# Group B's gates with features on partitions, applied behind the transposes; local and context scores of 256 keys in one product

## The chip, the cores and the metric

The kernel runs on one core of a Trainium2 chip. The metric is the device time of one execution in microseconds. A core has a matrix engine (TensorE, "PE" in the profile, with its weight loads as "PEld"), a vector engine (VectorE, "DVE"), an activation engine (ScalarE, "ACT"), a general engine (GpSimd, "POOL") and a queue for transfers (SyncE, "SP"). Matrix products are written to PSUM, which has eight banks of 128 x 512 float32; everything else lives in SBUF.

## The reference

Two layers of a transformer with three groups of attention heads side by side, over 512 latent tokens (a grid of 8 rows by 64 columns) and 256 context tokens, width 1024, head size 64, float32. Cut to what matters:

```python
px = split_cols(hx @ w_in)      # latent; hx is the normalised, modulated input
pc = split_cols(hc @ w_in)      # context, through the same weights
ya, yca = global_gqa(...)          # A: 8 heads, all latent keys and all context keys
yb, ycb = neighbourhood_attn(...)  # B: 8 heads, a clamped 8 x 16 window, a bias, and all context keys
yc_, ycc = window_gqa(...)         # C: 8 heads, keys within 128 tokens, a sink logit, all context keys
ux = jnp.concatenate([ya, yb, yc_], axis=-1) * jax.nn.silu(px[9])
x = x + gate[:, None, :] * (ux @ w_out)
if need_ctx:                       # first layer only
    uc = jnp.concatenate([yca, ycb, ycc], axis=-1) * jax.nn.silu(pc[9])
    cx = cx + gate_c * (uc @ w_out)
```

`px[9]` and `pc[9]` are 1536 columns of gates, 512 for each group. The second layer makes nothing for the context beyond its keys and values.

## The kernel before, in words

Products are made of two rounded halves of every operand, high and low, three products for each (high with high, high with low, low with high), so that float32 accuracy remains. The weights come in pieces of 256 KB on SP's queue; ACT rounds the high half (`split`, L242), DVE or POOL subtracts for the low one (L245).

There are two forms of projection. `proj_t` puts 128 tokens on the partitions of the result: the stationary operand is a tile of 128 tokens, the moving one a weight block of 256 columns, 24 products of 256 columns for a tile, two tiles in a bank (L336). `proj_f` puts 128 features on the partitions: the weights are stationary, the tokens move, 24 products of 512 columns for the latent part and 24 of 256 for the context (L313). Weight blocks are numbered in two tables, `wt` and `wf` (`col_index`).

Heads are worked in pairs (12 pairs, four in each group). `PLAN` lists stages: in each, the attention of one pair is woven on TensorE with the projections that later pairs need (`weave`, with a rough cost for each kind in `time`). Stage `("B", 3)`, for instance, runs attention of B's last pair beside the projections `akv` and `a` 0, and stage `("A", 0)` runs A's first pair beside `ckv` and `c` 0. The instructions so written get a priority by their order, and a planner, with its own estimate of times, fixes the order on every engine and gives each tile a buffer when its first writer is placed; a tile waits until the former holder of its buffer is done. On the chip every engine then follows that order. Projections use two PSUM banks, `pj`, one after the other.

Attention of a pair is made of units, one head each (`NearUnit` in B, `BandUnit` in C, `GlobalUnit` in A, `CtxUnit` for context queries). For a tile of 128 queries a unit makes two products with the context keys and two with the local keys (the high and low half of the keys), into one region of `Sbig`; then DVE adds the bias and finds the maximum, ACT takes the exponential, TensorE transposes the probabilities into `T`, ACT and DVE split them (L793, L1039), and TensorE multiplies them with the values into `Obig`. In `NearUnit` query tiles 1 and 2 have 256 local keys, tiles 0 and 3 have 192. In `BandUnit` tiles 0 and 3 have 256, tiles 1 and 2 have 384.

`finish(c)` ends a pair, in the next stage, behind the last unit's values. It needs the gates (the factor 0.5 of the tanh form is applied there):

- groups A and B: the gates G have tokens on partitions. POOL multiplies G in place with the reciprocal of the softmax sums (L1315, one instruction for each tile of 128 tokens), TensorE transposes, and DVE multiplies the transposed product with the attention output OT into u (L1332).
- group C: the gates (`c_g`) have features on partitions. POOL multiplies a constant of ones with the reciprocals into a tile R in the slot `tR` (L1315), TensorE transposes, DVE multiplies OT with it in place (L1326), and POOL multiplies with G into u (L1328, L1330).

u is then stored by a transfer from ACT's queue (L1340), except for the last three. Slot `tR` has one buffer. It also holds the rotated K and Q of group C (`rope_c`: L966, L974, L976) and group C's V before its transposes (L1001, L1003).

B's gates before: `b_g(m)` makes the gates of two pairs at once by `proj_t`, with a tanh on ACT and a product on DVE for each half bank (`g_silu`, L874, L875).

Of the kernel before, what the change touches and what calls it, by code (L numbers as in the profile page):

```python
# [21 lines left out]
NT = 512  # L22
NCX = 256
NA = NT + NCX
# [5 lines left out]
RPAD = 32  # L30
FT_ORDER = (4, 5, 6, 7, 0, 8, 1, 9, 2, 10, 3, 11)

PLAN = [(None, [("g", 0), ("b", 0), ("v", 0)], (0, 18)),
# [15 lines left out]

CFG = dict(lead=6.0, hp=600, hpf=600, pj=2, T=2, O=1, P=5, qt=5, kt=4, vt=4, gt=3, wh=5, ws=3, pt=3, bm=2, tA=1, OT=1, u=1, tl=1, ab="pj", tR=1, map={}, ada=2, h0=300, h1=1000, a0=9, H=2, hr=0, cp="A", cv="A", w0="D", w1="D", w2=(("D", "D"), ("D", "D")), hb="D", ws_="P")  # L50

WT_A_KV, WT_A, WT_BV, WT_BG = 0, 1, 5, 7
WF_BQ, WF_BK, WF_CQ, WF_CK, WF_CV, WF_CG = 0, 4, 8, 12, 13, 14

SM_C, SM_NW, SM_AB, SM_FW = 0, 16, 32, 80
SM_N = 88
# [710 lines left out]
def mixers(tc, nc, l, last, p1, ps, const, env):  # L767
# [6 lines left out]
    nq = 4 if last else 6  # L774
    ncol = nq * 128
    need_cq = not last
# [7 lines left out]
    def newG():  # L784
        return slot("gt")
# [149 lines left out]
        yield from proj_t(l, WT_BV + m, 6, bank, done, g_["off_tile"])  # L935
        return V

    def b_g(m, bank):
        G = [newG() for _ in range(2)]

        def done(p, t2):
            for x in range(2):
                g_silu(G[x], p, t2, x * 128)

        yield from proj_t(l, WT_BG + m, nq, bank, done)
        return G

    def tables_c():
        for c in range(2):
# [63 lines left out]

    def c_g(i, bank):

        G = p1.tile([128, NA], F32, name="gc", tag="bm", bufs=CFG["bm"])

        def done(p, c0, n):
            th = p1.tile([128, NT], F32, name="th", bufs=1)
            nc.scalar.activation(th[:, 0:n], p, AF.Tanh, scale=0.5)  # L1020
            nc.vector.scalar_tensor_tensor(G[:, c0:c0 + n], th[:, 0:n], 1.0, p, op0=OP.add, op1=OP.mult)

        yield from proj_f(l, WF_CG + i, need_cq, bank, done)
        return G

    def c_pair(i, bank):
        Q = yield from c_q(i, bank)
# [15 lines left out]
    def mul(*args, **kw):  # L1043
        m = nc.tensor.matmul(*args, **kw)  # L1044
        pace["pe"] = m.ins.name
        return m
# [24 lines left out]
    def sbank():  # L1071

        k = third["n"] = (third["n"] + 1) % 3
        return Sbig[:, k * 512:(k + 1) * 512]

    class Unit:

# [86 lines left out]
    class BandUnit(Unit):  # L1164
        def scores(self):
            self.P, self.pos = {}, {}

            place = {1: (128, 128, 512), 2: (768, 1024, 768), 0: (0, 0, 256), 3: (1024, 1280, 1024)}
            for pair in ((1, 2), (0, 3)):
                for i in pair:  # L1170
                    ks = KS[i]
                    nl = 128 * len(ks)
                    s0, loc, cx = place[i]
                    q = self.Q[:, i * 128:(i + 1) * 128]
                    for x in range(2):
                        mul(Sbig[:, cx:cx + 256], q, self.K[:, x, NT:NA],
                                         start=(x == 0), stop=(x == 1), skip_group_check=True)
                        mul(Sbig[:, loc:loc + nl], q, self.K[:, x, ks[0] * 128:ks[0] * 128 + nl],
                                         start=(x == 0 and nl > 256), stop=(x == 1), skip_group_check=True)
                    yield (nl + 256) * 2 / 2400  # L1180
                for i in pair:
                    ks = KS[i]
                    s0, loc, cx = place[i]
                    n = 128 * len(ks) + 256
                    nm = self.stat("negm", i)
                    P = newP()
                    nc.vector.tensor_tensor_reduce(out=P[:, 0:n], in0=Sbig[:, s0:s0 + n], in1=self.bm()(i),  # L1187
                                                   op0=OP.add, op1=OP.min, scale=-1.0,
                                                   scalar=self.sink if self.sink is not None else 3.0e38, accum_out=nm)
# [23 lines left out]
    class NearUnit(Unit):  # L1213
# [9 lines left out]
        def scores(self):  # L1223
            self.P = {}
            for i in (1, 2, 0, 3):
                k0, p0, loc, cx, _ = self.PLAN[i]
                nl = min(256, NT - k0, 128 * i + 192)
                S = sbank()
                q = self.Q[:, i * 128:(i + 1) * 128]
                for x in range(2):  # L1230
                    a = mul(S[:, cx:cx + 256], q, self.K[:, x, NT:NA], start=(x == 0), stop=(x == 1),
                                         skip_group_check=True)
                    b = mul(S[:, loc:loc + nl], q, self.K[:, x, k0:k0 + nl], start=False,
                                         stop=(x == 1), skip_group_check=True)
                    if x == 0:
                        after(b, a.ins.name)
                yield (nl + 256) * 2 / 2400
                n = nl + 256
                nm = self.stat("negm", i)
                P = newP()  # L1240
                if n < 512:
                    z = 0 if p0 else n
                    nc.gpsimd.memset(P[:, z:z + 64], 0.0)
# [50 lines left out]
    def finish(c):  # L1294
# [8 lines left out]
                nc.vector.tensor_add(sums[:, h * 6:h * 6 + nq], sums[:, h * 6:h * 6 + nq], ex[:, h * 6:h * 6 + nq])  # L1303
        rec = p1.tile([128, 2, 6], F32, name="rec", bufs=2)
        nc.vector.reciprocal(rec[:, :, 0:nq], sums.rearrange("p (h t) -> p h t", h=2)[:, :, 0:nq])
        if kind == "C":
            R = slot("tR")
        else:
            R = G
# [1 line left out]
        u = slot("u")  # L1311
        ft = {"A": 0, "B": 4, "C": 8}[kind] + i
        for t in range(nq):
            src = onesw[:, None, :].to_broadcast([128, 2, 64]) if kind == "C" else R[:, t]
            en("fin").tensor_mul(R[:, t], src, rec[:, :, t:t + 1].to_broadcast([128, 2, 64]))  # L1315
        yield 0
        for c0, n in ((0, 4), (4, nq - 4)):
            if not n:
                continue
            T = psT()  # L1320
            for t in range(n):
                turn(T[:, t * 128:(t + 1) * 128],
                                    R[:, c0 + t].rearrange("p h f -> p (h f)"), ident)
            a, b = c0 * 128, (c0 + n) * 128
            if kind == "C":
                nc.vector.scalar_tensor_tensor(OT[:, a:b], OT[:, a:b], 0.5, T[:, 0:b - a], op0=OP.mult, op1=OP.mult)  # L1326
                if c0 == 0:
                    nc.gpsimd.tensor_mul(colmajor(u[:, 0:NT]), rowmajor(OT[:, 0:NT]), colmajor(G[:, 0:NT]))  # L1328
                else:
                    nc.gpsimd.tensor_mul(u[:, a:b], OT[:, a:b], G[:, a:b])  # L1330
# [160 lines left out]

    first = any_bank
    made = {}
    time = dict(akv=15.7, a=15.7 * nq / 6, ckv=15.7, c=2 * tq, b=7.8 + tq, v=15.7, g=15.7 * nq / 6)
    make = dict(akv=lambda i, bank: a_kv(bank), a=a_pair, ckv=lambda i, bank: c_kv(bank), c=c_pair, b=b_qk, v=b_v,
                g=b_g)

# [7 lines left out]
    for pair, items, n_ada in PLAN:  # L1505
        if pair is None and not last:

            items = items[1:] + items[:1]
        if pair is not None:
            kind, i = pair  # L1510
            if kind == "B":
                Q, K = made["b", i]
                prev = units("B", i, Q, K, made["v", i // 2][i % 2], lambda i=i: made["g", i // 2][i % 2], bmb)
# [33 lines left out]
def col_index():  # L1547
# [6 lines left out]
    wt += [3072 + 512 + i * 256 + r(256) for i in range(2)]  # L1554
# [4 lines left out]
    wf += [3072 + 1024 + i * 128 + r(128) for i in range(4)]  # L1559
    return wt, wf  # L1560


# [80 lines left out]
```

## Time and profile before

| | |
|---|---|
| median of 3 runs | 1206.64 us (1205.81 to 1206.85) |
| profiled execution | 1206.79 us |
| its span, first to last instruction | 1204.9 us |
| TensorE busy | 1159.1 us, 96%, 8016 products |
| DVE busy | 766.0 us, 64% |
| ACT busy | 697.7 us, 58% |
| POOL busy | 418.3 us, 35% |
| mean granted TensorE clock | 0.995 |

The busy time of an engine is the time in which at least one of its instructions runs. Products overlap, so the mean duration of one says less than the distance between starts in a run without interruption. "Idle before" tells what ended an empty stretch. A line such as `Sbig<-kt,qt` names the tile written and the tiles read.

### The profile page before, as it was taken

How to read it: one execution, taken by the hardware profiler on the slowest of the kernel's cores; microseconds unless marked ns; L12 is line 12 of the kernel's file. 1: busy time of each engine (PE TensorE's matmuls, PEld its weight loads, DVE VectorE, ACT ScalarE, POOL GpSimd, SP SyncE). 2: the span in 40 equal slices, each digit the busy share in tenths (PEclk: the TensorE clock that was granted, in tenths of full speed). 3: DMA queues.
4: the chain of work that ended last, by engine and by line, in shares of the span. 5: the costliest groups of instructions: out<-in, count | busy, mean ns of one | idle time of the engine just before them, and what ended most of it. 6: DMA issues, size and time to landing. Idle time of an engine off the chain costs nothing.

```text
span 1204.9 us, 21753 instructions
## 1 busy us (share of the span) xinstructions
PE 1159.1 (96%) x8016; PEld 1037.9 (86%) x8016; DVE 766.0 (64%) x1541; ACT 697.7 (58%) x1581; POOL 418.3 (35%) x511
## 2 busy tenths in 40 slices
PE   5999999999999999999999999999999999989997
PEld 3898999998888989988878999989989888878876
DVE  5767566764556656568577895576755655557553
ACT  5446555655656576588423543554666766667552
POOL 1441110234447354376110030212365554546001
PEclk9999999999999999999999999999999999999998
DMA  8552222312223112124086662332321202132152
GB/s 328 203 141 89 78 77 75 121 64 95 80 94 100 54 56 78 49 62 119 27 305 205 196 199 75 94 105 83 106 67 57 68 30 71 36 88 80 35 158 79
DMA packets 60826, 124.22 MB, mean 103 GB/s; under 512 B 7216, under 2 KB 13488, under 8 KB 60720
## 3 DMA queue, kind: packets, MB, share of 16 engines
q1 hardware_dynamic: 54768, 111.96, 29.2%
q10 hardware_dynamic: 5952, 10.88, 2.7%
q8 instruction: 63, 1.03, 0.3%
q14 instruction: 43, 0.35, 0.1%
HBM read 109.05 MB, written 11.14 MB: 100 GB/s over the span
## 4 chain that ended last, share of the span: by engine, by line
PE 83%; DVE 6%; ACT 4%; DMA 3%; issue 3%; POOL 0%; ACTq 0%; SPq 0%; DVEq 0%; POOLq 0%
PE pj L313 19%; PE pj L336 17%; PE Sbig L1044 10%; PE Obig L1044 9%; PE T L1049 9%; PE pj L514 4%; PE T L514 3%; PE Sbig L514 3%; PE T L336 2%; PE Sbig L425 1%; DVE ptl L1039 1%; ACT pth L793 1%; PE pj L425 1%; PE Sbig L336 1%; PE pj L209 1%
## 5 line engine op out<-in xcount | busy, mean ns | idle before, releaser
L1039 DVE TENSOR_TENSOR ptl<-T,pth 128x512 fp32r<-128x512 f32 (+2 forms) x312 | 181.3, 591 | 126.8 <-ACT pth L793 124.9
L793 ACT ACTIVATE pth<-T 128x512 fp32r<-128x512 f32 (+2 forms) x312 | 158.8, 519 | 136.4 <-PE T L1049 123.4
L336 PE MATMUL pj<-wh,hL 128*128 128x256 f32 x896 | 180.0, 287 | 0.1
L313 PE MATMUL pj<-hL,wh 128*128 128x512 f32 x544 | 176.3, 402 | 1.0 <-ACT wh L242 0.6
L1049 PE MATMUL T<-ident,P 128*128 128x128 f32 x1024 | 165.8, 274 | 5.9 <-DVE ptl L1039 3.7
L242 ACT ACTIVATE wh<-ws 128x512 fp32r<-128x512 f32 x192 | 119.6, 629 | 80.9 <-PE pj L313 13.9
L1044 PE MATMUL Sbig<-kt,qt 128*128 128x256 f32 (+1 forms) x864 | 157.0, 309 | 0.9 <-DVE negm L1187 0.7
L245 POOL TENSOR_TENSOR wl<-ws,wh 128x512 fp32r<-128x512 f32 x76 | 98.4, 1300 | 154.3 <-ACT wh L242 141.2
L336 PEld LDWEIGHTS pj<-wh,hL 128*128 128x128 f32 x896 | 144.2, 191 | 2.5 <-issue 0.6
L1049 PEld LDWEIGHTS T<-ident,P 128*128 128x128 f32 x1024 | 123.0, 140 | 19.9 <-DVE ptl L1039 3.9
L1044 PE MATMUL Obig<-pth,vt 128*128 128x256 f32 (+2 forms) x432 | 133.2, 319 | 6.0 <-ACT pth L793 5.2
L1044 PE MATMUL Obig<-ptl,vt 128*128 128x256 f32 (+2 forms) x432 | 132.1, 320 | 3.6 <-DVE ptl L1039 3.1
L1044 PEld LDWEIGHTS Sbig<-kt,qt 128*128 128x128 f32 x864 | 123.7, 190 | 10.2 <-DVE negm L1187 2.2
L336 PE MATMUL pj<-wl,hL 128*128 128x256 f32 x448 | 128.5, 287 | 0.0
L245 DVE TENSOR_TENSOR wl<-ws,wh 128x512 fp32r<-128x512 f32 x116 | 85.2, 741 | 43.3 <-ACT wh L242 39.4
L313 PEld LDWEIGHTS pj<-hL,wh 128*128 128x128 f32 x544 | 96.6, 190 | 17.1 <-ACT wh L242 1.0
L313 PE MATMUL pj<-hL,wl 128*128 128x512 f32 x272 | 107.4, 395 | 0.6 <-DVE wl L245 0.6
L1044 PEld LDWEIGHTS Obig<-pth,vt 128*128 128x128 f32 x432 | 81.9, 190 | 16.6 <-ACT pth L793 9.6
L1044 PEld LDWEIGHTS Obig<-ptl,vt 128*128 128x128 f32 x432 | 81.8, 189 | 14.7 <-DVE ptl L1039 9.6
L1419 POOL TENSOR_TENSOR bm<-wr,bm 128x192 f32<-128x192 f32 (+1 forms) x48 | 40.8, 881 | 142.2 <-DMA bm<-mskB_dram 134.8
L336 PEld LDWEIGHTS pj<-wl,hL 128*128 128x128 f32 x448 | 85.4, 191 | 0.4
L1139 DVE TENSOR_REDUCE negm<-Sbig 128x1 f32<-128x768 f32 x64 | 61.1, 955 | 33.3 <-ACT P L1141 18.2
(334 smaller groups left out, 2510.5 us busy)
## 6 DMA issues: line engine op xcount, KB each, us to landing
ws<-wf_dram SPq DMA_DIRECT2D x72, 256.0 KB, 2.9
ws<-wt_dram SPq DMA_DIRECT2D x72, 256.0 KB, 2.9
ada<-adaw_dram SPq DMA_DIRECT2D x32, 512.0 KB, 5.1
ws<-wo_dram SPq DMA_DIRECT2D x57, 256.0 KB, 2.8
bm<-mskB_dram SPq DMA_DIRECT2D x16, 576.0 KB, 3.9
dw<-adat_dram SPq DMA_DIRECT2D x8, 512.0 KB, 7.3
dots<-adat_dram SPq DMA_DIRECT2D x16, 256.0 KB, 4.1
u<-u ACTq DMA_DIRECT2D x9, 384.0 KB, 3.1
```

Source lines behind the costliest of these rows:

```text
L242: nc.scalar.activation(hi, src, AF.Copy)
L245: eng.tensor_sub(lo, src, hi.bitcast(F32))
L313: paced(nc.tensor.matmul(p[:, 0:n], a[:, r, :], cols(b[kt], c0, n), start=(i == 0), stop=(i == 23)), i)
L336: paced(nc.tensor.matmul(p[:, t * 256:(t + 1) * 256], tok(a[kt], t2 + t), b[:, r, :], start=(i == 0), stop=(i == 23)), i)
L425: mm = nc.tensor.matmul(out, a, b, start=begin, stop=(kt == KT - 1 and i == 2), skip_group_check=True)
L514: mm = nc.tensor.matmul(p[:, 0:n], a[:, r, :], ucols(ua[b][ft], c0, n), start=(ft == FT_ORDER[0] and i == 0), stop=(ft == FT_ORDER[-1] and ...
L793: nc.scalar.activation(out, src, AF.Copy)
L1039: i = nc.vector.tensor_sub(lo[:, 0:n], T[:, 0:n], hi[:, 0:n].bitcast(F32))
L1044: m = nc.tensor.matmul(*args, **kw)
L1049: m = nc.tensor.transpose(*args, **kw)
L1139: nc.vector.tensor_reduce(nm, S, axis=AX.X, op=OP.max, negate=True)
L1419: nc.gpsimd.tensor_add(b, src, b)
```

## The change: what it does

1. `b_g(i)` makes the gates of one pair by `proj_f`, as group C does, from four new weight blocks of 128 features (`WF_BG`) in place of two blocks of 256. ACT's tanh and DVE's product are now one each for 512 latent columns and one each for the 256 context columns. `PLAN` names `g` 0 and 1 in the first stage and 2 and 3 in stage `("B", 2)`.
2. `finish` treats B as it does C: ones times reciprocals into R in the slot `tR`, transposes, OT times R in place on DVE, then u = OT times G on POOL, with plain column order.
3. Where a query tile has 256 local keys, the local and the context keys are read by one product of 512 columns, through an access pattern of two runs of 256 (`beside`). This concerns tiles 1 and 2 of `NearUnit` and tiles 0 and 3 of `BandUnit`; in tile 3 of the latter the second run lies before the first.

```diff
-PLAN = [(None, [("g", 0), ("b", 0), ("v", 0)], (0, 18)),
+PLAN = [(None, [("g", 0), ("g", 1), ("b", 0), ("v", 0)], (0, 18)),
...
-        (("B", 2), [("b", 3), ("g", 1)], (0, 0)),
+        (("B", 2), [("b", 3), ("g", 2), ("g", 3)], (0, 0)),
...
-    def b_g(m, bank):
-        G = [newG() for _ in range(2)]
-
-        def done(p, t2):
-            for x in range(2):
-                g_silu(G[x], p, t2, x * 128)
-
-        yield from proj_t(l, WT_BG + m, nq, bank, done)
+    def gate_f(G, s, bank):
+        def done(p, c0, n):
+            th = p1.tile([128, NT], F32, name="th", bufs=1)
+            nc.scalar.activation(th[:, 0:n], p, AF.Tanh, scale=0.5)
+            nc.vector.scalar_tensor_tensor(G[:, c0:c0 + n], th[:, 0:n], 1.0, p, op0=OP.add, op1=OP.mult)
+
+        yield from proj_f(l, s, need_cq, bank, done)
         return G
+
+    def b_g(i, bank):
+        return (yield from gate_f(newG(), WF_BG + i, bank))
...
+    def beside(k, k0, k1):
+        return bass.AP(tensor=k.tensor, offset=k.offset + k0, ap=[k.ap[0], [k1 - k0, 2], [1, 256]])
...  # BandUnit.scores
+                        if nl == 256:
+                            k0 = ks[0] * 128
+                            mul(Sbig[:, s0:s0 + 512].rearrange("p (a b) -> p a b", a=2), q,
+                                beside(self.K[:, x], *((k0, NT) if loc < cx else (NT, k0))),
+                                start=(x == 0), stop=(x == 1), skip_group_check=True)
+                            continue
...  # NearUnit.scores
+                    if nl == 256:
+                        mul(S[:, 0:512].rearrange("p (a b) -> p a b", a=2), q, beside(self.K[:, x], k0, NT),
+                            start=(x == 0), stop=(x == 1), skip_group_check=True)
+                        continue
...  # finish
-        if kind == "C":
+        if kind in "BC":
             R = slot("tR")
...
-            src = onesw[:, None, :].to_broadcast([128, 2, 64]) if kind == "C" else R[:, t]
+            src = onesw[:, None, :].to_broadcast([128, 2, 64]) if kind in "BC" else R[:, t]
...
-            if kind == "C":
+            if kind in "BC":
                 nc.vector.scalar_tensor_tensor(OT[:, a:b], OT[:, a:b], 0.5, T[:, 0:b - a], op0=OP.mult, op1=OP.mult)
-                if c0 == 0:
+                if c0 == 0 and kind == "C":
                     nc.gpsimd.tensor_mul(colmajor(u[:, 0:NT]), rowmajor(OT[:, 0:NT]), colmajor(G[:, 0:NT]))
...
-    time = dict(akv=15.7, a=15.7 * nq / 6, ckv=15.7, c=2 * tq, b=7.8 + tq, v=15.7, g=15.7 * nq / 6)
+    time = dict(akv=15.7, a=15.7 * nq / 6, ckv=15.7, c=2 * tq, b=7.8 + tq, v=15.7, g=tq)
...
-            items = items[1:] + items[:1]
+            items = items[2:] + items[:2]
```

`c_g` calls `gate_f` too, with nothing else changed; `col_index` and the shapes of `wt` and `wf` follow (7 and 22 blocks in each layer, 9 and 18 before).

More of the change, by code (lines that the diff above doesn't have):

```diff
@@ L50 @@
 CFG = dict(lead=6.0, hp=600, hpf=600, pj=2, T=2, O=1, P=5, qt=5, kt=4, vt=4, gt=3, wh=5, ws=3, pt=3, bm=2, tA=1, OT=1, u=1, tl=1, ab="pj", tR=1, map={}, ada=2, h0=300, h1=1000, a0=9, H=2, hr=0, cp="A", cv="A", w0="D", w1="D", w2=(("D", "D"), ("D", "D")), hb="D", ws_="P")
-WT_A_KV, WT_A, WT_BV, WT_BG = 0, 1, 5, 7
-WF_BQ, WF_BK, WF_CQ, WF_CK, WF_CV, WF_CG = 0, 4, 8, 12, 13, 14
+WT_A_KV, WT_A, WT_BV = 0, 1, 5
+WF_BQ, WF_BK, WF_CQ, WF_CK, WF_CV, WF_CG, WF_BG = 0, 4, 8, 12, 13, 14, 18
 SM_C, SM_NW, SM_AB, SM_FW = 0, 16, 32, 80
@@ L1014, in c_g @@
     def c_g(i, bank):
[L1016 to L1024, printed above, removed]
+        return (yield from gate_f(p1.tile([128, NA], F32, name="gc", tag="bm", bufs=CFG["bm"]), WF_CG + i, bank))
     def c_pair(i, bank):
@@ L1512, in mixers @@
                 Q, K = made["b", i]
-                prev = units("B", i, Q, K, made["v", i // 2][i % 2], lambda i=i: made["g", i // 2][i % 2], bmb)
+                prev = units("B", i, Q, K, made["v", i // 2][i % 2], lambda i=i: made["g", i], bmb)
             else:
@@ L1553, in col_index @@
     wt += [1792 + i * 256 + r(256) for i in range(2)]
-    wt += [3072 + 512 + i * 256 + r(256) for i in range(2)]
     wf = [768 + i * 128 + r(128) for i in range(4)]
@@ L1559, in col_index @@
     wf += [3072 + 1024 + i * 128 + r(128) for i in range(4)]
+    wf += [3072 + 512 + i * 128 + r(128) for i in range(4)]
     return wt, wf
@@ L1616 @@
     w4 = w_in.reshape(2, 8, 128, 4608).transpose(0, 2, 1, 3)
-    wt = np.ascontiguousarray(np.stack([w4[..., i] for i in it], 1).reshape(2, 9, 128, 2, 4, 256)
-                              .transpose(0, 1, 3, 2, 4, 5)).reshape(2, 9, 2, 128, 1024)
-    wf = np.ascontiguousarray(np.stack([w4[..., i] for i in jf], 1)).reshape(2, 18, 128, 1024)
+    wt = np.ascontiguousarray(np.stack([w4[..., i] for i in it], 1).reshape(2, 7, 128, 2, 4, 256)
+                              .transpose(0, 1, 3, 2, 4, 5)).reshape(2, 7, 2, 128, 1024)
+    wf = np.ascontiguousarray(np.stack([w4[..., i] for i in jf], 1)).reshape(2, 22, 128, 1024)
     wo = np.ascontiguousarray(w_out.reshape(2, 3, 4, 128, 8, 128).transpose(0, 4, 1, 3, 2, 5)).reshape(
```

## The prediction, made before the result

> **What bounds the kernel now.** I read the page first, then busy time by stretch, then the order of work on TensorE. The page's first part and its chain of work:
>
> ```profile
> span 1204.9 us, 21753 instructions
> PE 1159.1 (96%) x8016; PEld 1037.9 (86%) x8016; DVE 766.0 (64%) x1541; ACT 697.7 (58%) x1581; POOL 418.3 (35%) x511
> PE 83%; DVE 6%; ACT 4%; DMA 3%; issue 3%; POOL 0%; ACTq 0%; SPq 0%; DVEq 0%; POOLq 0%
> ```
>
> TensorE is busy 96% of the span and holds 83% of the chain. The stretches where the change works (a middle pair of group B, then the stage after the last pair of B, in layer 0 and layer 1):
>
> ```profile
> core 0: us, PE busy (x) PEld busy (x) DVE busy (x) ACT busy (x) POOL busy (x), PEclk, DMA share, GB/s
> 116.00:164.00 48.00, 48.00 (x355) 45.44 (x354) 31.36 (x66) 26.89 (x65) 7.70 (x16) 1.00 0.27 84
> 262.00:313.00 51.00, 51.00 (x324) 43.40 (x324) 26.69 (x48) 28.86 (x64) 25.96 (x24) 1.00 0.29 91
> 875.00:925.00 50.00, 49.20 (x313) 43.48 (x312) 26.89 (x48) 30.36 (x64) 25.67 (x24) 1.00 0.22 69
> ```
>
> In the first, TensorE has no empty moment (48.00 of 48) at full clock, while DVE, ACT and POOL have 16, 21 and 40 us to spare. So a stage of group B is worth what its matmuls cost to issue, and nothing that only lightens DVE, ACT or POOL moves the end. A matmul's own duration is no price, since neighbours overlap; the price is the spacing in an unbroken run. Three runs from the chain, and four score products from the order of work on TensorE:
>
> ```profile
> 80.53 5.76 PE pj L336 x48
> 86.77 5.47 PE pj L313 x24
> 1169.03 15.87 PE pj L514 x70
> ...
> 137.80 0.64 PE L1044 MATMUL Sbig<-kt,qt 128*128 128x256 f32 x4
> 138.28 0.28 PE L336 MATMUL pj<-wh,hC 128*128 128x256 f32 x1
> ```
>
> 48 products of 256 columns (L336) take 5.76 us: 120 ns each. 24 of 512 columns (L313) take 5.47 us: 228 ns; I use 229 to allow for the start of a run, and 15.87/70 = 227 ns (L514) is the best case. The score products of 256 are also (138.28 - 137.80)/4 = 120 ns. Two products of 256 put into one of 512 save 240 - 229 = 11 ns: that is all the change has to give on TensorE.
>
> **The change part by part.** *Gates of group B, products.* Before, one weight block of 256 features costs 24 products of 256 columns for each tile of 128 tokens: two blocks by 6 tiles in layer 0 and by 4 in layer 1 are 288 + 192 = 480 products, 57.6 us at 120 ns. After, four blocks of 128 features cost 24 products of 512 columns each in both layers, and 24 of 256 for the context in layer 0: 192 x 0.229 + 96 x 0.120 = 55.5 us. Saved: 192 x 11 ns = 2.1 us, all of it where TensorE has no slack. The columns streamed are the same 122,880; only the number of products falls.
>
> *Scores.* In group B tiles 1 and 2 of each unit have 256 local keys, in group C tiles 0 and 3; 16 units in each group over both layers make 64 such tiles, each going from four products (0.480 us) to two (0.458): 1.4 us saved. The trace has no product whose moving operand comes in two pieces. Products that write two pieces (the last keys of a B unit) sit at the same 117 to 123 ns spacing as their neighbours where nothing waits, so I take no surcharge; the bounds are 227 ns each (1.7 us saved) and 240 (nothing).
>
> The skill speaks against both savings. By the Trainium skill, "TensorE: Matmul & The Clock Gate", section Back-to-back issue gap, a warm product is spaced by its columns over 2.4 GHz and 2.5 ns: 109.2 ns for 256 columns, 215.8 for 512, so a merge would save 2.5 ns and 320 merges 0.8 us, an estimate from that page, in place of 3.5. The rows above (120, and 228 or 227) lie above both figures and differ from twice the smaller by 11 ns or more, so the sum goes by the rows.
>
> *Gate evictions.* Rows of the lines that make group A's and B's gates (874, 875) and C's (1020, 1021):
>
> ```profile
> L874 ACT ACTIVATE th<-pj x32: 363/383/408, 86.3 to 1068.5; 128x256 f32<-128x256 f32 x32
> L875 DVE SCALAR_TENSOR_TENSOR gt<-th,pj x32: 402/416/422, 87.5 to 1068.9; 128x256 f32<-128x256 f32 x32
> L1020 ACT ACTIVATE th<-pj x12: 366/590/618, 317.2 to 1103.8; 128x512 f32<-128x512 f32 x8, 128x256 f32<-128x256 f32 x4
> L1021 DVE SCALAR_TENSOR_TENSOR gc<-th,pj x12: 410/677/690, 317.9 to 1104.4; 128x512 f32<-128x512 f32 x8, 128x256 f32<-128x256 f32 x4
> ```
>
> Twenty pairs of 256 become eight of 512 and four of 256: ACT 20 x 0.383 = 7.7 to 6.2 us, DVE 20 x 0.416 = 8.3 to 7.1. Both engines have spare time here, so zero; without that cover it is at most 2.7 us.
>
> *The gate behind the transposes.* The six (four) multiplications of L1315, the transposes and the DVE product stay as many; their source becomes ones. New on POOL: 8 products of 512 columns and 4 of 256. Rows of C's same step, and POOL around a B pair's end:
>
> ```profile
> L1328 POOL TENSOR_TENSOR u<-OT,gc x8: 1538/1563/1581, 379.7 to 1151.6; 128x512 f32<-128x512 f32 x8
> L1330 POOL TENSOR_TENSOR u<-OT,gc x4: 742/750/769, 382.4 to 604.1; 128x256 f32<-128x256 f32 x4
> ...
> 120.04 2.41 POOL L1315 TENSOR_TENSOR gt<-gt,rec 128x128 f32<-128x128 f32 x6
> 127.31 0.26 POOL L1243 MEMSET P<- 128x64 f32 x2 [4.86 <-PE T L1049]
> 139.38 2.65 POOL L1419 TENSOR_TENSOR bm<-wr,bm 128x192 f32<-128x192 f32 x3 [11.81 <-DMA bm<-mskB_dram]
> ```
>
> 8 x 1.56 + 4 x 0.75 = 15.5 us at most, on an engine idle 40 of 48 us. Behind a waiting product in POOL's queue stand the next memsets of P and bias fill; from 127.57 to 139.38 the queue is empty, and that is where transposes and products fall. The store of u waits in ACT's queue, with weight copies behind it, and becomes ready 0.75 to 2.3 us later. I take zero, since TensorE has other work; 8 x 2.3 = 18 us is an outer bound, if every hold reached TensorE uncovered.
>
> *Moved steps.* Gates are made in the same stages, per pair instead of per two pairs. Weight pieces (8 per layer, 256 KB each, on SP's queue), their splits, and the banks they cycle through are as many. At layer 1's start the first gate needs two pieces where it needed four: zero, bounded by a microsecond either way.
>
> *The new claim on slot tR.* The reciprocals now stand in tR, which has one buffer, instead of in the gate's own tile. For pairs 0 to 2 of B nobody else wants tR. The last pair's finish, however, runs while group C's K and V are projected, and their rotated K, then V, live in tR too. Layer 0, then layer 1:
>
> ```profile
> 263.21 2.21 POOL L1315 TENSOR_TENSOR gt<-gt,rec 128x128 f32<-128x128 f32 x6 [0.36 <-DVE rec L1305]
> 275.77 0.38 ACT L966 ACTIVATE tR<-pj 128x256 f32<-128x256 f32 x1 [0.19 <-PE pj L313]
> 287.14 0.38 PE L1049 MATMUL T<-ident,gt 128*128 128x128 f32 x2
> 289.33 1.12 ACT L1003 ACTIVATE tR<-pj 128x512 f32<-128x512 f32 x1
> ...
> 894.97 2.20 POOL L1315 TENSOR_TENSOR gt<-gt,rec 128x128 f32<-128x128 f32 x4
> 897.18 1.10 ACT L1003 ACTIVATE tR<-pj 128x512 f32<-128x512 f32 x1 [0.32 <-POOL gt L1315]
> 903.71 0.60 PE L1049 MATMUL T<-ident,gt 128*128 128x128 f32 x4
> ```
>
> In layer 0 the reciprocals hold tR from 263.2 until the last transposes at 287.5; K's context eviction, done at 275.8 today, must wait 11.7 us and keeps one of two projection banks (pj). V's latent part fills the other until about 285, so projections lose the time from there to 288, 2 to 3 us, and V's eviction comes later than 289.3. In layer 1 the slot goes from K to the reciprocals at 895; V's eviction waits from 897.2 to 904.3, 7 us, then both banks are shut and the next projection cannot begin. What TensorE loses without projections, from a stretch where it has attention alone:
>
> ```profile
> 366.74 0.28 PE L313 MATMUL pj<-hC,wl 128*128 128x256 f32 x1
> 371.00 0.45 PE L1044 MATMUL Obig<-pth,vt 128*128 128x384 f32 x1 [0.27 <-ACT pth L793]
> 373.34 0.44 PE L1044 MATMUL Obig<-ptl,vt 128*128 128x384 f32 x1 [0.33 <-DVE ptl L1039]
> 374.83 0.48 PE L313 MATMUL pj<-hC,wh 128*128 128x256 f32 x2
> ...
> 380.11 0.44 PE T L1049 x4
> ...
> 282.79 1.02 PE L209 MATMUL pj<-ada,silu_c 128*2 128x256 f32 x10
> ```
>
> Between 366.86 and 374.83 it issues eight scores of 256 columns (0.96 us), 18 transposes (at 110 ns from the row of four, at most 2.0) and 12 value products of 256 to 512 columns (priced by columns at the spacings above, about 2.1): 5 of 8 us, so 0.38 us lost per us. The 7 us of layer 1 cost 2.7. For layer 0 I take zero: the 2 to 3 us in question hold modulation products (L209) today, two columns of weights each, which can go later; its ends are 0 and 11.7 x 0.38 = 4.4. Together 2.7, between 0 and 7.1.
>
> **Sum**, against the profiled execution's 1206.8 us (span 1204.9 and 1.9 around it; 0.15 above the median of the runs): -2.1 - 1.4 + 2.7 = -0.8, so 1206.0, and 1205.8 as a median.
>
> **The rivals.** *The slot costs nothing (faster).* Today's transposes come long after the multiplications have ended (265.4 to 287.1, and 897.2 to 903.7), so there is room to issue them sooner, and attention work can be drawn forward. Against it: TensorE follows an order fixed beforehand, in which this lag stands. Then -3.5: 1203.1; with 227 ns per product, 13 ns x 320 = 4.2, 1202.4.
>
> *The slot costs its full price (slower).* Both holds leave TensorE with attention alone: 7.1 - 3.5 = +3.6, 1210.2. It decides once the slot costs more than 3.5 + 2.4 = 5.9 us, that is 15.5 us without projections out of the 18.8 held. For it: three tiles in a row (reciprocals, K, V) pass through one buffer. Against: in layer 0 one bank stays open for most of the hold.
>
> *The change does not do what it says.* A product of 512 columns costs two of 256, from a moving operand in two pieces or from counting columns alone: nothing saved, the slot paid, 1206.6 + 2.7 = 1209.3. Against it stand the spacings above, for it only that no two-piece read exists in this trace. The Trainium skill's formula, named above, is nearly this case: with its 0.8 us it would be 1208.5.
>
> **How the numbers follow.** A measurement of this kernel tells about 0.2% (2.4 us) from no change: 1204.2 to 1209.1 is "same". Forecast (the slot eats most of the saving) 0.37: its share is 0.04 faster, 0.31 same, 0.02 slower. Slot free 0.33: 0.31 faster, 0.02 same. Slot at full price 0.18: 0.17 slower, 0.01 same. No saving 0.12: half same, half slower. Sums: faster 0.35, same 0.40, slower 0.25. The range goes from 1202 (slot free, best spacing) to 1210.5 (full price); the forecast's own range is 1204 to 1208.
>
> **What would show it.** In the changed kernel's trace: L313's successor in runs of 24 products of 512 for the gates at 228 to 230 ns; merged scores at two per tile and about 230 ns; POOL some 13 to 15 us busier with TensorE's busy share in B's stages unchanged; and, decisive, whether the evictions into tR after the last pair of B stand later than today behind the transposes of the reciprocals, with TensorE empty there. The forecast is wrong if these evictions do not move, if merged scores are spaced at 240 ns or more, or if a stage without any of these steps changes its length by more than a microsecond.

## The result, and the profile after

The changed kernel takes 1214.24 us (median of 6 runs, 1212.64 to 1216.62) against 1206.79 us (6 runs, 1205.81 to 1208.88) for the kernel before, run beside it: ratio 1.0064, 95% interval 1.0051 to 1.0077. It is 7.5 us slower, above the range that was given. The profiled execution took 1215.45 us. Its page:

```profile
span 1213.6 us, 21110 instructions
PE 1159.3 (96%) x7696; PEld 1021.5 (84%) x7696; DVE 768.4 (63%) x1533; ACT 695.9 (57%) x1573; POOL 432.3 (36%) x523
PE 80%; DVE 7%; ACT 4%; issue 4%; DMA 3%; POOL 1%; SPq 0%; ACTq 0%; DVEq 0%; POOLq 0%
```

TensorE issues 320 products fewer (7696 for 8016) and POOL works 14.0 us more, both as forecast; TensorE's share of the chain falls from 83% to 80%, in favour of DVE and issue. In busy time by stretch, the first three rows answer to the three shown of before; the fourth is where layer 1 begins:

```profile
core 0: us, PE busy (x) PEld busy (x) DVE busy (x) ACT busy (x) POOL busy (x), PEclk, DMA share, GB/s
116.00:164.00 48.00, 48.00 (x344) 44.91 (x343) 31.31 (x66) 27.24 (x67) 9.69 (x18) 1.00 0.29 83
262.00:313.00 51.00, 49.91 (x325) 43.05 (x323) 29.30 (x53) 31.69 (x69) 27.73 (x25) 1.00 0.26 81
...
690.00:700.00 10.00, 7.52 (x22) 5.50 (x21) 6.91 (x17) 4.56 (x11) 0.70 (x1) 0.69 0.46 145
...
875.00:925.00 50.00, 47.17 (x295) 40.66 (x294) 31.71 (x54) 32.05 (x71) 28.15 (x25) 1.00 0.19 64
```

In B's middle TensorE is still full (48.00 of 48). At 690 us it issues 22 products in 10 us, at a granted clock of 0.69. The same 10 us of the kernel before:

```profile
690.00:700.00 10.00, 9.34 (x67) 8.47 (x66) 8.86 (x22) 5.99 (x16) 1.13 (x1) 1.00 0.54 163
```

**A ledger of TensorE.** For each product I take the undisturbed spacing of its shape (229 ns for 512 columns, 178 for 384, 120 for 256, 90 for 192, 108 for a transpose) as work, and what is left of a stretch as loss. The kernel before has 1126.3 us of work and 78.7 of loss in its span of 1204.9. The stretches are cut at the reciprocals that open each pair's `finish` and at the last product of layer 0's output. Differences to the kernel before, in us, one profiled execution each:

```
                                  work  loss: layer 0  layer 1    B's    B's end,  rest    span
                                                       begins     pairs  layer 1
after                             -3.5          3.5      5.7       1.1     3.0    -1.1     8.6
scores only (e1)                  -1.4          2.2      0.7       0.3     2.5    -0.4     4.0
gates only (e2)                   -2.1          2.2      7.3       0.5     5.8     0.4    14.1
after, R in u (e3)                -3.5          2.0      5.7       1.5     0.6    -0.4     6.0
after, old gates in part (e4)     -3.0          3.3     -1.6       1.3     3.0     1.1     4.2
e4 and R in u (e5)                -3.0          2.7      1.7       1.1     0.4     0.1     3.0
after, four pieces first (e9)     -3.5          0.8     -0.9       2.3     3.0    -0.5     1.2
e9 and R in u (e10)               -3.5          5.1      3.7       0.8     0.4     1.2     7.7
e10, old scores (e11)             -2.1          0.1      4.4       0.5    -0.6     0.4     2.7
e9, old scores (e17)              -2.1          3.7     -0.1       0.7     4.4     1.0     7.6
```

The work fell by the 3.5 us that had been forecast. The loss grew by 12.2, of which 5.7 stand at layer 1's start and 3.0 at B's end in layer 1. One caution: `after` and e9 have the same order of work on every engine through layer 0, and their executions differ there by 2.7 us, so that column, and the last digits of any, are scatter between executions (e9's profiled one took 1207.93 us, 2.5 below its median). Part of the 2.7 is the granted clock: between 370 and 380 us it is 0.83 in the changed kernel's execution and 1.00 in e9's.

**Where layer 1 begins.** Order of work on TensorE in the changed kernel (start, duration, line, what it waited for; `hL` is the layer's input for the latent tokens, `wh` and `wl` are the halves of a weight piece):

```profile
688.20 0.63 PE L313 MATMUL pj<-hL,wh 128*128 128x512 f32 x2
688.66 0.39 PE L313 MATMUL pj<-hL,wl 128*128 128x512 f32 x1
688.89 0.62 PE L313 MATMUL pj<-hL,wh 128*128 128x512 f32 x2
689.34 0.39 PE L313 MATMUL pj<-hL,wl 128*128 128x512 f32 x1
689.57 0.62 PE L313 MATMUL pj<-hL,wh 128*128 128x512 f32 x2
690.02 0.39 PE L313 MATMUL pj<-hL,wl 128*128 128x512 f32 x1
692.26 0.73 PE L313 MATMUL pj<-hL,wh 128*128 128x512 f32 x2 [1.85 <-ACT wh L242]
693.63 0.96 PE L354 MATMUL Obig<-ones,sq 128*128 128x2 f32 x4 [0.63 <-DVE sq L350]
694.45 0.77 PE L313 MATMUL pj<-hL,wl 128*128 128x512 f32 x1
695.02 1.05 PE L313 MATMUL pj<-hL,wh 128*128 128x512 f32 x2
...
700.56 0.62 PE L313 MATMUL T<-hL,wh 128*128 128x512 f32 x2
```

Up to 690.02 the products start every 228 ns (eight in 1.82 us). Then two stalls, 2.0 us and 0.8 us, and from 694.45 a slow stretch: until 700.56 thirteen products and two transposes take 6.1 us, one product every 427 ns, where they would take 3.2. The stall cost 2.8 us, the clock after it 2.9 more. The Trainium skill, "TensorE: Matmul & The Clock Gate", section Back-to-back issue gap, gives 512 columns over 1.2 GHz for the slowed clock, 427 ns; the trace agrees.

The first stall waits for a weight half from ACT, and yet the weight piece is not late: it was issued at 678.17, and no piece from there to 700 us took more than 3.5 us to land. In ACT's queue it stood behind a part of the input that DVE had not yet made:

```profile
690.88 0.26 ACT L288 ACTIVATE hL<-hL 128x64 fp32r<-128x64 f32 x1 [1.41 <-DVE hL L595]
691.28 0.42 ACT L346 ACTIVATE sq<-xn 128x256 f32<-128x256 f32 x1
691.60 0.61 ACT L242 ACTIVATE wh<-ws 128x512 fp32r<-128x512 f32 x1
```

The second stall waits for DVE itself (L350). Why DVE is late is seen in SP's queue and on DVE. The kernel before, SP:

```profile
664.20 2.81 SPq L251 DMA_DIRECT2D ws<-wt_dram  x3
...
669.40 0.33 SPq L251 DMA_DIRECT2D ws<-wt_dram  x1
...
670.25 1.86 SPq L143 DMA_DIRECT2D dots<-adat_dram  x4
```

and DVE:

```profile
670.23 1.41 DVE L582 SCALAR_TENSOR_TENSOR xn<-xn,mod,rbl 128x512 f32<-128x512 f32 x2
...
676.50 0.75 DVE L153 CUSTOM_DVE_ANT_0 junk<-dots,sm 128x512 bf16<-128x512 f32 x1 [1.00 <-DMA dots<-adat_dram]
```

The changed kernel, SP:

```profile
665.91 0.93 SPq L251 DMA_DIRECT2D ws<-wf_dram  x2
...
667.36 1.85 SPq L143 DMA_DIRECT2D dots<-adat_dram  x4
```

and DVE:

```profile
673.84 0.75 DVE L153 CUSTOM_DVE_ANT_0 junk<-dots,sm 128x512 bf16<-128x512 f32 x1 [2.76 <-DMA dots<-adat_dram]
...
675.46 1.41 DVE L582 SCALAR_TENSOR_TENSOR xn<-xn,mod,rbl 128x512 f32<-128x512 f32 x2
...
695.43 0.74 DVE L595 SCALAR_TENSOR_TENSOR hL<-xn,mod,hL 128x512 fp32r<-128x512 f32 x1
```

`dots` are operands of layer 1's modulation sums (L153), eighteen steps strewn through layer 1's first stage. The first step follows the first products of that stage. The first gate used to need four weight pieces before it yielded; now it needs two, so the transfers of `dots` are issued behind two pieces, and the planner puts the first L153 on DVE's queue ahead of L582, which makes layer 1's input. Its transfer lands late, DVE stands still for 2.76 us with the input queued behind it, and the first L582 comes at 675.46 where it came at 670.23 (the changed kernel runs 1.7 us later there). The last part of the input (L595) comes about 8 us after layer 0's last product, where it came about 6.

### The profile page after: what moved, and what is told of

It is laid out like the page before. It is cut to its first block, busy times and chain, and to the rows that moved or that the text cites. A ratio compares the mean times of both kernels' runs of the same rounds, so it can differ in the third digit from the quotient of the medians.

```text
span 1213.6 us, 21110 instructions
## 1 busy us (share of the span) xinstructions
PE 1159.3 (96%) x7696; PEld 1021.5 (84%) x7696; DVE 768.4 (63%) x1533; ACT 695.9 (57%) x1573; POOL 432.3 (36%) x523
## 4 chain that ended last, share of the span: by engine, by line
PE 80%; DVE 7%; ACT 4%; issue 4%; DMA 3%; POOL 1%; SPq 0%; ACTq 0%; DVEq 0%; POOLq 0%
PE pj L313 21%; PE pj L336 14%; PE Sbig L1040 10%; PE Obig L1040 9%; PE T L1045 8%; PE pj L514 4%; PE T L514 3%; PE Sbig L514 2%; PE Sbig L425 1%; PE T L313 1%; DVE ptl L1035 1%; ACT pth L793 1%; DMA dots<-adat_dram 1%; PE pj L425 1%; PE Sbig L336 1%
## 5 line engine op out<-in xcount | busy, mean ns | idle before, releaser
L313 PE MATMUL pj<-hL,wh 128*128 128x512 f32 x624 | 203.2, 404 | 3.8 <-ACT wh L242 2.4
L336 PE MATMUL pj<-wh,hL 128*128 128x256 f32 x768 | 156.5, 288 | 0.1
L313 PEld LDWEIGHTS pj<-hL,wh 128*128 128x128 f32 x624 | 111.5, 190 | 23.4 <-ACT wh L242 3.3
L336 PEld LDWEIGHTS pj<-wh,hL 128*128 128x128 f32 x768 | 124.8, 190 | 3.0 <-issue 0.6
L313 PE MATMUL pj<-hL,wl 128*128 128x512 f32 x312 | 124.2, 399 | 0.0
L1040 PEld LDWEIGHTS Sbig<-kt,qt 128*128 128x128 f32 x736 | 110.7, 190 | 13.1 <-DVE negm L1193 2.5
L336 PE MATMUL pj<-wl,hL 128*128 128x256 f32 x384 | 109.5, 285 | 0.0
L313 PE MATMUL pj<-hC,wh 128*128 128x256 f32 x384 | 75.7, 290 | 0.0
```

Of the source, the lines that this page charges most:

```text
L313: paced(nc.tensor.matmul(p[:, 0:n], a[:, r, :], cols(b[kt], c0, n), start=(i == 0), stop=(i == 23)), i)
L336: paced(nc.tensor.matmul(p[:, t * 256:(t + 1) * 256], tok(a[kt], t2 + t), b[:, r, :], start=(i == 0), stop=(i == 23)), i)
```

## The experiments

**The two halves of the change.** e1 is the kernel before with only the scores' products merged (`beside` and its two uses); e2 is the changed kernel with those two uses taken out.

> The kernel before with the merged score products alone (64 tiles, two products of 512 columns for four of 256); gates and finish as before. Every theory puts the loss elsewhere. If a merged product is spaced at 229 to 235 ns: 0.3 to 1.4 us faster than before, 1205.4 to 1206.5. If a moving operand in two pieces costs two products: no change, spacing 240 ns.

Measured: 1209.12 us (9 runs) against 1205.40; the two sets of runs are compared as a whole, ratio 1.0023 (1.0010 to 1.0036), where the medians alone give 1.0031. Both branches of the expectation missed: it is slower.

> The changed kernel with the scores as before (four products of 256): gates by features, applied behind the transposes. Both theories (boundary: the loss arises where layer 1 begins; slot: it arises where the last pair of B and group C want slot tR) keep all of the loss here: 1214 to 1216, some 1 us above the changed kernel.

Measured: 1217.21 us, ratio 1.0097 (1.0077 to 1.0116), above the 1214 to 1216 that both theories gave, so it does not separate them. The merged scores made one kernel 0.23% slower and the other 0.33% faster. The gates carry the loss.

**The slot tR.** e3 puts B's reciprocals into u, which is free until u itself is made:

```diff
-        if kind in "BC":
+        u = slot("u")
+        if kind == "B":
+            R = u
+        elif kind == "C":
             R = slot("tR")
```

> The changed kernel with group B's reciprocals R put into the tile of u itself (free until u is written, behind the transposes) in place of slot tR. Theory boundary: no change, 1213 to 1215, and layer 1's first reciprocal at about 778 us as now. Theory slot: the 3.6 us that the trace shows between the end of B and the first pairs of A and C in layer 1 go, 1210 to 1211; if the slot were the whole cause, 1204 to 1206.

Measured: 1214.41 us, ratio 1.0068 (1.0052 to 1.0084): the total did not move. Yet what the slot did is plain in POOL's waits at B's end in layer 1 (us in total, times, longest), in the changed kernel:

```profile
POOL tR L978 <- PE T L1045: 7.1, 1, 7.1
```

and in e3:

```profile
POOL tR L978 <- ACT tA L972: 1.8, 1, 1.8
```

K's rotation (L978) waited 7.1 us for the transposes of the reciprocals, and with R in u it no longer does. In the ledger the loss at B's end is 3.0 with tR and 0.6 with u.

**Old gates where layer 1 begins.** e4 is the changed kernel with layer 1's first two B pairs on the old gates (a block of 256 features, multiplied before the transposes); e5 is e4 with R in u.

> The changed kernel, but in layer 1 pairs 0 and 1 of B have their gates made and applied as before (tokens on partitions, weight block of 256 features); all else changed. Theory boundary: the 5 to 7 us lost between the end of layer 0 and the first attention of layer 1 go, 1207 to 1209, and no stretch of half clock stands there. Theory slot: no change, 1213 to 1215, as pair 3 of B still uses slot tR.

Measured: 1211.36 us, ratio 1.0047 (1.0031 to 1.0063), between the ranges of the two theories. The ledger's loss at layer 1's start goes from +5.7 to -1.6.

> The changed kernel with B's R in the slot u, and with layer 1's first two B pairs on the old gates (256 features per block, multiplied before the transposes). Both long stretches should go: 1203 to 1208. If it stays above 1210, neither the start of layer 1 nor the slot is what makes the changed kernel slower.

Measured: 1208.38 us (12 runs), ratio 1.0018 (1.0005 to 1.0030), just above the range, and still slower than the kernel before.

**The modulation sums one stage later.** The 18 steps moved from layer 1's first stage to `("B", 0)`, in the changed kernel (e6), in the kernel before (e7) and in e3 (e8):

```diff
-PLAN = [(None, [("g", 0), ("g", 1), ("b", 0), ("v", 0)], (0, 18)),
-        (("B", 0), [("b", 1)], (0, 0)),
+PLAN = [(None, [("g", 0), ("g", 1), ("b", 0), ("v", 0)], (0, 0)),
+        (("B", 0), [("b", 1)], (0, 18)),
```

> The changed kernel, with layer 1's modulation sums (the 18 products L153 and their transfers) issued in stage ("B", 0) instead of in the stage in which layer 1 begins. Theory DVE: where layer 1 begins DVE is full, and in the changed kernel it stands 4 us behind the transfer of one of these operands before it makes the last parts of the layer's input; TensorE then runs out of weight halves and inputs and loses its clock. Then the stretch between layer 0's output and the first finish of B in layer 1, 5.2 us longer in the changed kernel, loses 4 to 6 us, the granted clock in the 10 us after the start stays at 1.00, and the median falls to 1208 to 1211. Theory weights (the gates' order of weight pieces alone starves TensorE there): that stretch keeps its 5 us and the median stays at 1213 to 1215.

> Control: the kernel before with the same move of the 18 products L153. Theory DVE: the kernel before lost only about 1 us to that transfer, so 0 to 2 us faster than before, 1204.5 to 1207. If the move is worth more than 3 us here too, it is a gain of its own and does not explain the difference between the kernels.

> The changed kernel with both: B's R in the slot u instead of tR, and the 18 products L153 one stage later. If the start of layer 1 (5 us) and the slot in layer 1 (5 us) are two separate causes, both go: 1202 to 1207. If the total is set by something else that shifts from stage to stage, it stays above 1210.

Measured: 1215.00 (1.0087), 1215.02 (1.0078, 1.0054 to 1.0101) and 1214.98 us (1.0077). All three medians lie outside what theory DVE and the two causes had given (the 4 us in e6's expectation are the 2.76 us of the row above). The move costs the kernel before 9 us by itself (3.9 us of loss among B's pairs of layer 1, 2.4 at layer 1's start), so against the kernel before it settles nothing. Against e7, which has the same move, e6 does say something on the cause. Its medians are equal, and the ratios differ by 0.09% (uncertain by 0.35). The stretch where layer 1 begins is 84.0 us long in e6 and 83.2 in e7, 0.8 us apart, where the changed kernel's is 5.2 us longer than that of the kernel before. TensorE's waits between 685 and 745 us are the same two in e6 and in e7:

```profile
PE T L373 <- POOL rstd L364: 0.4, 1, 0.4
PE pj L313 <- ACT wh L242: 0.3, 1, 0.3
```

The clock is 1.00 in both around 695 us. So without the sums in that stage the new gates, still with two pieces ahead, bring no more stall there than the old ones. Theory weights had e6's median right (1213 to 1215) but wanted the longer stretch, and it is gone. The move says one thing more: the place of 18 small steps of DVE is worth as much as the whole difference under study.

**Four pieces first.** e9 undoes one thing: in layer 1 the pieces of gates 0 and 1 are fetched together, ahead of the first gate's products.

```diff
     def proj_f(l, s, need_ctx, bank, done):
-        w = None if banks else load_wf(l, s)
+        w = None if banks else both.pop(s, None) or load_wf(l, s)
...
     def b_g(i, bank):
+        if last and i == 0: g_["both"].update((s, g_["load_wf"](l, s)) for s in (WF_BG, WF_BG + 1))
         return (yield from gate_f(newG(), WF_BG + i, bank))
```

> The changed kernel with one thing undone: at the start of layer 1 the four weight pieces of gates 0 and 1 are fetched ahead of the first gate's products, as the kernel before fetched its four pieces. The transfers of the modulation sums (dots) then stand behind four pieces in SP's queue instead of two, and DVE's first L153 behind the first two L582 instead of ahead of them; nothing before that point changes its place on any engine. Theory order (DVE waiting behind that L153 delays layer 1's input, TensorE stalls and its clock drops): DVE's wait for dots near 672 us falls below 1.5 us, the granted clock in the 10 us around 695 is 1.00, the stretch from layer 0's output to B's first finish is at most 1 us longer than before, and the median falls by 3 to 5 us, to 1209 to 1211.5. Theory form (the features-on-partitions products need all eight input parts early, whatever DVE does): no change, 1213 to 1215.

Measured: 1210.46 us (11 runs), ratio 1.0035 (1.0023 to 1.0047), 3.8 us below the changed kernel. SP in e9's profile:

```profile
668.45 0.33 SPq L251 DMA_DIRECT2D ws<-wf_dram  x1
...
669.30 1.85 SPq L143 DMA_DIRECT2D dots<-adat_dram  x4
```

DVE:

```profile
669.27 1.41 DVE L582 SCALAR_TENSOR_TENSOR xn<-xn,mod,rbl 128x512 f32<-128x512 f32 x2
...
674.86 0.75 DVE L153 CUSTOM_DVE_ANT_0 junk<-dots,sm 128x512 bf16<-128x512 f32 x1 [0.31 <-DMA dots<-adat_dram]
```

and busy time in the 10 us around 695:

```profile
690.00:700.00 10.00, 9.93 (x46) 7.95 (x45) 8.87 (x22) 6.55 (x14) 1.13 (x1) 1.00 0.42 134
```

Both L582 stand ahead of L153 again, which waits 0.31 us; the clock is 1.00. Theory form is out: the products are the same features-on-partitions products, and TensorE's order of work is that of the changed kernel until long after the stall (up to 705.8 us of the changed kernel's profile). By itself e9 also fetches pieces earlier; that their lateness was not the cause is shown by ACT's queue above and by e6 beside e7. The ledger's loss at the start goes from +5.7 to -0.9.

**Both mended, and the scores undone.** e10 is e9 with R in u, e11 is e10 with separate scores, e17 is e9 with separate scores.

> The kernel of e9 with B's R in the slot u as well. If the two causes add as the old gates of layer 1 suggested (1211.4 with the start alone mended, 1208.4 with both), the median is 1207 to 1209.5. If the slot costs nothing once the start is mended, it equals e9 within 1 us.

> The kernel of e10 with the scores in separate products as before: the gates' change alone, with both causes mended. If the merged scores cost time of their own (1209.1 against 1205.4 when only they were changed), 1204 to 1207. If the price of 11 ns per merge holds and the rest is the order of work, about e10 + 1.4, with 3 us either way from the order.

> The kernel of e9 with the scores in separate products: the gates' change alone, with layer 1's start mended. If the merged scores carry the rest, as in the kernel before with merged scores alone (2.8 us), 1206.5 to 1208.5. If the gates carry it, 1210 to 1212 or, by the 11 ns per merge, 1.4 us above e9. If merged scores gain in this kernel as they did in the changed one (3 us), 1213 to 1214.

Measured: 1212.36 (1.0046, 1.0033 to 1.0059), 1211.12 (1.0034, 1.0021 to 1.0048) and 1214.59 us (1.0053, 1.0034 to 1.0072). e10 missed: the slot's loss is gone (0.4), but with R in u another order of work follows layer 1's start, and weight pieces are late there (ACT waits 3.1 us for them in e10 and 3.6 in e11, between 690 and 745 us). e11 lies in its second range, and e17 above all of its ranges. TensorE's longest wait between 690 and 745 us in e11:

```profile
PE pj L313 <- ACT wh L242: 3.8, 2, 3.2
```

Merged against separate scores in four settings: +0.23% (e1), -0.33% (after to e2, reversed), +0.12% (e10, e11), -0.18% (e9, e17), each uncertain by 0.13 to 0.23%. On average nothing; the 0.1% that the ledger's work gives cannot be told from it.

**Other orders of work.** `lead` is how far projections may run ahead of attention when the order is written out. It was changed in the kernel before and in e9, with the same work:

```diff
-CFG = dict(lead=6.0, ...
+CFG = dict(lead=6.4, ...
```

> Control: the kernel before with lead 6.4 in place of 6.0, the constant by which projections may run ahead of attention when the order of work is written out; same work, same products, another order on every engine. If a mere reordering moves this kernel by some us, 1207 to 1214, and the 2 to 3 us that merged scores or mended gates leave are of that size. If the order hardly matters, 1205 to 1207, and those 2 to 3 us need a cause of their own.

> The kernel before with lead 5.6 in place of 6.0: same work, another order. Theory order: like lead 6.4 (1217.8) this leaves a good order, 1208 to 1218. If 6.4 was an unlucky case, 1205 to 1208.

> The kernel before with lead 5.8. Theory order: 1207 to 1215; otherwise 1205 to 1207.

> The kernel of e9 (the change with the start of layer 1 mended) with lead 5.6. Theory order: away from the lead for which the kernel before had its good order, the change is no longer behind: within 3 us of the kernel before with lead 5.6, ahead as likely as behind. Theory own cost: 2 to 6 us slower than the kernel before with lead 5.6.

> The kernel of e9 with lead 5.8. Theory order: within 3 us of the kernel before with lead 5.8, ahead as likely as behind. Theory own cost: 2 to 6 us slower than it.

> The kernel of e9 with lead 6.4, against the kernel before with lead 6.4 (1217.8). Theory own cost (the work saved on TensorE comes back as waiting, with some us more): 1218 to 1222. Theory order: anywhere between 1210 and 1226, ahead as likely as behind.

Measured, as ratios to the kernel before as it is:

```
lead    kernel before               e9 (change, start mended)   difference
5.6     1.0145 (1.0124 to 1.0166)   1.0157 (1.0137 to 1.0176)   0.12%
5.8     1.0070 (1.0055 to 1.0086)   1.0099 (1.0074 to 1.0123)   0.29%
6.0     1                           1.0035 (1.0023 to 1.0047)   0.35%
6.4     1.0085 (1.0071 to 1.0099)   1.0093 (1.0078 to 1.0107)   0.08%
```

Every other lead costs the kernel before 8 to 17 us, above the range that a mere reordering had been given each time (1217.75 us at 6.4, 1224.29 at 5.6, 1215.59 at 5.8). At each lead the mended change is behind, by 2.5 us on average; only at 6.0 does a pair's difference stand clear of its uncertainty (0.2 to 0.3% at the other three). The two theories are not separated: theory order allowed all of it but had put ahead as likely as behind, and theory own cost holds at 5.8 and 6.4 but not at 5.6, where the difference is 1.8 us.

## Why the prediction was wrong

**Moved steps: the step that failed.** "At layer 1's start the first gate needs two pieces where it needed four: zero, bounded by a microsecond either way." The fact was the right one, the price was not. It cost 3.8 of the 7.5 us (after to e9: 0.29%, uncertain by 0.18), in two further pairs 0.44% (e2 to e17, uncertain by 0.27) and 0.22% (e3 to e10, uncertain by 0.21). I priced the pieces and not what is queued behind them: fewer pieces ahead bring the next transfers and DVE's first L153 forward in the order. The windows show DVE full where layer 1 begins (10.00 of 10 us between 680 and 690 us in the kernel before):

```profile
680.00:690.00 10.00, 9.38 (x66) 8.45 (x64) 10.00 (x23) 5.97 (x16) 0.00 (x0) 1.00 0.45 141
```

I had read DVE's spare time in B's middle and not here. For the same reason "all of it where TensorE has no slack" is wrong for the gates made here: TensorE already stood waiting at this place in the kernel before (9.34 of 10 us busy between 690 and 700). The prediction's own sign for being wrong, "a stage without any of these steps changes its length by more than a microsecond", is nearly what happened: a stage in which I had put the step at zero grew by 5.2 us. None of the rivals held such a stall, so neither did the range.

**Products: right.** TensorE's work fell by 3.5 us. The gates' products are spaced at 228 to 230 ns; a merged score takes 230 where nothing waits (the median over all products of that line and shape, merged or not, is 234):

```profile
119.48 0.40 PE L1040 MATMUL Sbig<-kt,qt 128*128 128x512 f32 x1
119.71 0.40 PE L1040 MATMUL Obig<-pth,vt 128*128 128x512 f32 x1
119.94 0.39 PE L1040 MATMUL Sbig<-kt,qt 128*128 128x512 f32 x1
120.17 0.28 PE L336 MATMUL pj<-wl,hL 128*128 128x256 f32 x1
```

So a moving operand in two pieces costs nothing extra, and the rival that a merge saves nothing is out. What was wrong is that saved work shortens the span: the loss beside it took it back.

**The slot: mechanism right, price borne out by the ledger but not by the medians.** In the changed kernel's layer 0, K's context eviction (L970) starts at 285.4, right behind the transposes, and TensorE lost nothing by it, as put:

```profile
L1325 POOL TENSOR_TENSOR tR<-onesw,rec x6: 399/403/585, 266.4 to 268.6; 128x128 f32<-128x128 f32 x6
...
L1045 PE MATMUL T<-ident,tR x6: 271/272/273, 282.4 to 284.8; 128*128 128x128 f32 x6
...
L970 ACT ACTIVATE tR<-pj x1: 384/384/384, 285.4 to 285.4; 128x256 f32<-128x256 f32 x1
```

In layer 1 a wait of 7.1 us was there where 7 had been worked out, though it was K that waited, not V, since the reciprocals now took the buffer first. Its price in the ledger is 3.0 us three times, and 5.8 and 4.4 with separate scores, where R is in tR; with R in u it is -0.6 to 0.6 four times. 2.7 had been put. That column also moves by 2.5 (e1) from order alone. In the medians R in u gained 0.29% once (e4 to e5, uncertain by 0.20) and 0.19% (e17 to e11, where R in u is the only change; uncertain by 0.23), and nothing or less twice (after to e3, e9 to e10). e10 lost more at layer 1's start (3.7 against -0.9) than it gained here. For e3 the two measures disagree: its profiled execution is 2.8 us faster than the changed kernel's (1212.68 against 1215.45), and the medians are equal. So what the slot costs in the total stays open.

**POOL and evictions at zero: nothing speaks against it.** No run prices the evictions alone. The new products on POOL, 13.8 us, lie where it was idle:

```profile
L1340 POOL TENSOR_TENSOR u<-OT,gt 128x512 f32<-128x512 f32 x8 | 10.8, 1355 | 40.5 <-DVE OT L1336 40.5
...
L1340 POOL TENSOR_TENSOR u<-OT,gt 128x256 f32<-128x256 f32 x4 | 3.0, 740 | 8.4 <-DVE OT L1336 8.4
```

**What stays open.** With the start mended the sum of my steps still stands at -0.8 us, and the kernel at +2.5 on average over four leads, +3.6 at its own. These 3 to 4 us are not settled. Between the two kernels at the same lead the ledger shows 1.1 to 3.0 us more loss among B's pairs of layer 1, at all four leads, where the work fell by 0.8 to 2.0; no single wait of TensorE carries it (at lead 6.0 its waits there come to 1.3 us in e9 and 0.3 in the kernel before), and with four orders a price of the change cannot be told from the luck of its order. The kernel before has the best order of those drawn: three other leads, the moved sums and the merged scores all made it slower. The range had no term for that, and it is the largest uncertainty of the case.

## What to carry to other kernels

Where a planner writes a fixed order, price an edit by what it moves in the queues, not only by what it adds: look for the place where the engine behind the bottleneck is itself full, and ask which late transfer now stands ahead of the work that everything waits for. Before such a kernel's change is judged, draw the unchanged kernel in a few other orders: here they cost 8 to 17 us, more than the change, so a gain of 3.5 us of issue work cannot be seen until the order is fitted anew. A short stall on TensorE may cost twice: 2.8 us of waiting brought 2.9 us of slowed clock.

## What the runs showed of the hardware

- The granted clock fell after two stalls of 2.0 and 0.8 us inside 3.4 us, with products between them, and stayed low for about 6 us of unbroken products (694.4 to 700.5). The Trainium skill, "TensorE: Matmul & The Clock Gate", section Why this matters for your kernels, warns of idle gaps beyond about 3 us; here no single gap was that long. In the kernel before, stalls of 0.62 and 0.59 us at the same place left the clock at 1.00.
- A moving operand in two runs of 256 columns is read at the pace of one run of 512: 230 ns from product to product.
- 18 modulation steps moved by one stage cost the kernel before 8.9 us (e7), though DVE, where they run, is busy 64% of the span.
- From one execution of the same program to the next the mean granted clock differs, and the time with it: of e9's eleven executions the fastest (1207.93 us) had 0.997, the two slowest (1212.77 and 1213.57 us) 0.990.
